# Dot products of the modulation held one behind each MLP unit, and four changes of where small and last data lie

## The chip, the core and the metric

The kernel runs on one core of one Trainium2 chip. The metric is the device time of one execution in microseconds (us), the median of several runs; lower is better. The core's engines each work through their own instructions in order: PE (TensorE, the matmuls), ACT (ScalarE), DVE (VectorE), POOL (GpSimd) and SP (SyncE), which here issues most of the DMA loads. The order of an engine's instructions is fixed when the program is built: a scheduler takes the instructions that the Python code traces and sets them one behind the other on each engine, by its own estimate of when each one's inputs are ready. An instruction whose input is late holds everything behind it on its engine.

## The reference: what is computed

Two layers of a token mixer and an MLP on x of 512 tokens by 1024, in fp32. What matters here:

```python
cond = silu(c)
for l in range(2):
    mod = cond @ mod_w[l] + mod_b[l]          # 1024 -> 6*1024
    shift1, scale1, gate1, shift2, scale2, gate2 = split(mod, 6)
    h = rms_norm(x, attn_pre_g) * (1 + scale1) + shift1
    y = mixers(h @ w_in) @ w_out              # sparse, retention, GLA and differential heads
    x = x + gate1 * rms_norm(y, attn_post_g)
    h = rms_norm(x, mlp_pre_g) * (1 + scale2) + shift2
    y = square(relu(h @ mlp_w1)) @ mlp_w2     # 1024 -> 4096 -> 1024
    x = x + gate2 * rms_norm(y, mlp_post_g)
```

## The kernel before

Each fp32 product is made of three matmuls (`mm3`) of a high and a low part: hi x hi, hi x lo, lo x hi. So every weight tile is loaded by SP into a ring of four buffers (`raw`), ACT rounds it into a high part (`act.copy`, line 267), and DVE or POOL subtracts that for the low part (line 268). `prep` does this; where the pair lies is set by the list `slots`, which is rotated: W6 is a pool of six pairs (`whi`, `wlo`) that lives through the whole kernel, WX ten pairs of a pool that is opened in `rest` (`xhi`, `xlo`) and closed at its end, WG eight pairs that share their place with the MLP's hidden tiles.

`mixers(l)` runs the input projections and the four head groups of layer l; at its start it opens a pool of ten pairs (`zh`, `zl`) on the side of the memory where WX was closed, and asks for the weights of the projections 3, 0 and 1, twelve tiles. `rest(l)` runs the output projection and the MLP. The MLP goes over the 4096 hidden columns in four quarters q. In a quarter there are eight hidden units f (24 matmuls of 512 columns each; quarter 0 has them in two halves of 256 tokens), each followed by relu (ACT), square (DVE, line 1325) and a split into high (ACT) and low (DVE) part in `hidden`; then eight output units (two column halves c by four token blocks b), each read out of PSUM by ACT (quarter 0) or added on DVE. The last quarter's output units come in an order of their own (`last`), and their weights are called `ws`: column half 0 from `slots`, column half 1 into the place of the MLP's input (`wr`). Behind each block of it come the post norm (`add_block`) and the norm ahead of the next layer (`norm_block`, `turn_half`).

The products `cond @ mod_w` are done on DVE: 96 dot products over 128 x 1024 (`gemv`, line 285), 16 at the start and 80 from a list `todo`, from which `fill(n)` takes n at a place in the program. Each loads 512 KB of `mod_w` (`gw`, two buffers) by SP. `fence` holds instructions behind which the dot products are set on DVE; in `rest` it holds the last subtraction of `turn_half`, from the beginning of the MLP on. All but eight of the 56 that layer 0's `rest` takes belong to layer 1, and all of them are done in layer 0. When the eighth of part 2 or 5 is done, `gain_out` turns the norm weights by PE (line 507), copies them to SBUF by ACT (line 509) into a buffer of the tag `sq`, and POOL issues a DMA of them to DRAM (line 510). The two `sq` buffers also serve `rope` (its products `r1` and `r2`), `headnorm` and `turn_half`.

Projection 3 gives keys, index keys, values, index weights and the GLA gate input; `ev_k` copies them out of PSUM with four ACT instructions a block, into `tmK`, `Va`, `wi` (scaled) and `ca`.

Of the kernel before, what the change touches and what calls it, by code (L numbers as in the profile page):

```python
# [10 lines left out]
F32 = mybir.dt.float32  # L11
# [4 lines left out]
ALU = mybir.AluOpType  # L16
# [73 lines left out]
P = 128  # L90
L = 2
DM = 1024
T = 512
KT = 8
NB = 4
# [103 lines left out]
def tile_trunk(ctx: ExitStack, tc: tile.TileContext, a, out, dbg=None):  # L199
    nc = tc.nc  # L200
    pe, act, dve, pool, sp = nc.tensor, nc.scalar, nc.vector, nc.gpsimd, nc.sync

    def bits(t):
        return t.bitcast(F32)
# [28 lines left out]
    ones = cp.tile([P, P], F32, name="ones")  # L233
# [13 lines left out]
    nt = ctx.enter_context(tc.tile_pool(name="nt", bufs=2))  # L247
# [5 lines left out]
    slots = [(wp, "whi", "wlo", WB)]  # L253
# [25 lines left out]
    fence = []  # L279
# [21 lines left out]
    def fill(n):  # L301
        for _ in range(min(n, len(todo))):
            todo.pop(0)()
# [157 lines left out]

    def split(v, hi, lo, eng=None):
        act.copy(hi, v)
        (eng or dve).tensor_tensor(lo, v, bits(hi), ALU.subtract)

    def h_tiles(name):
        a, b = (hp.tile([P, KT, T], F32R, name=f"{name}{s}", tag="h" + s, bufs=1) for s in "hl")
        whole[name] = (a, b)
        return [(a[:, i], b[:, i]) for i in range(KT)]
# [33 lines left out]
    def gain_out(l, which):  # L503

        gain(l, which)
        pt = tr.tile([P, T], F32, name=f"tg_{which}{l}", tag="tr")[0:KT, 0:P]
        pe.transpose(pt, gmul[l, which], ident)
        g = nt.tile([P, T], F32, name=f"gt_{which}{l}", tag="sq")[0:KT, 0:P]
        act.copy(g, pt)
        pool.dma_start(rows[2 * l + (which == "post2")], g)  # L510

# [95 lines left out]
    def mixers(l, h, ch):  # L607
# [38 lines left out]
        def pv_block(ps, b, ss, Vs, name):  # L646

            W = P * (b + 1)
            st = []
            for hh in range(2):  # L650
                pt = tr.tile([P, T], F32, name=f"tp{name}_{hh}", tag="tr")
                for j in range(b + 1):
                    pe.transpose(pt[:, P * j:P * j + P], ss[hh][:, P * j:P * j + P], ident)
                st.append(mx.tile([P, T], F32, name=f"pt{name}_{hh}", tag="PT", bufs=4))
                act.copy(st[hh][:, :W], pt[:, :W])
            for j in range(b + 1):
                for hh in range(2):
                    pe.matmul(ps[64 * hh:64 * hh + 64, b * P:(b + 1) * P], Vs[hh](j), st[hh][:, P * j:P * j + P],
                              start=(j == 0), stop=(j == b))
# [80 lines left out]
            ahead(3)  # L740


        Va = mx.tile([P, NB, 64], F32, name=f"Va{l}")
        wi = mx.tile([P, NB, 8], F32, name=f"wi{l}")
        ca = mx.tile([P, NB, 17], F32, name=f"ca{l}")
        pool.memset(ca[:, :, 16:], 1.0)
        tmK = [s0.tile([P, P], F32, name=f"tK{l}_{b}", tag="tK", bufs=4) for b in range(NB)]
        KS = mx.tile([P, 4, T], F32R, name=f"KS{l}")

        def ev_k(b, ps):  # L750
            act.copy(tmK[b][:, 0:128], ps[:, 0:128])
            act.copy(Va[:, b, :], ps[:, 128:192])
            act.mul(wi[:, b, :], ps[:, 192:200], 8 ** -0.5 * 64 ** -0.5)
            act.copy(ca[:, b, 0:16], ps[:, 200:216])

        def keys(b):
            rope(mx, tmK[b].rearrange("p (h d) -> p h d", d=64), "A", b, 2, f"K{l}_{b}", E[PLAN["kr"][b]])
# [317 lines left out]
        def a_block(pr, b):  # L1075
            if b:
                top(max(0, 16 * b + 1 - taken[0]))
            W = P * (b + 1)
            sb = []
            for hh in range(2):  # L1080
                nme = f"A{l}_{pr}_{hh}_{b}"
                ps = sc.tile([P, T], F32, name="s" + nme, tag="sc")
                two_pass(ps, QS[:, 2 * pr + hh, b * P:(b + 1) * P], 0, max(W, 256))
                s, rc = softmax_scores(ps[:, :W], masks[b], W, HD ** -0.5, nme)
                z = PLAN["xa"][4 * pr + b]
                xx = act.mul(s, s, rc) if z == "a" else E[z].tensor_scalar(s, s, rc, None, ALU.mult)
                if PLAN['fence']:
                    fence[:] = [xx]
                sb.append(s)
            yield  # L1090
            if b == 0:
                yh[pr] = yp.tile([P, T], F32, name=f"ya{l}_{pr}", tag="yp")
            pv_block(yh[pr], b, sb, [lambda j: Va[:, j, :]] * 2, f"A{l}_{pr}_{b}")
            if b == NB - 1:
                headnorm(pr, yh[pr])

# [171 lines left out]
    def rest(l, yv):  # L1268
# [12 lines left out]
        row = gain_row(l, "post1")  # L1281
        gain(l, "pre2")
        if l == 0:
            gemv_list((0, 5), *[(1, part) for part in range(6)])
        slots[:] = [W6] * 6 + [WG] * 8 + [WX] * 2
        wo = [[None] * KT for c in range(2)]
        for c in range(2):
# [33 lines left out]
        def hidden(ps, hid, c, name):  # L1321
            n = c.stop - c.start
            rl = nt.tile([P, T], F32, name=f"rf{name}", tag="rs", bufs=RS)[:, :n]
            act.activation(rl, ps, AF.Relu)  # L1324
            dve.tensor_tensor(rl, rl, ps, ALU.mult)  # L1325
            split(rl, hid[0][:, c], hid[1][:, c])

        full = slice(0, T)
        for q in range(4):
            hid = [tuple(ml.tile([P, T], F32R, name=f"hd{l}_{q}_{f}{s}", tag="g" + s, bufs=8) for s in "hl")  # L1330
                   for f in range(8)]
            ws = [None] * 8
            for half in range(2 if q == 0 else 1):
                c = cs(half) if q == 0 else full
                for f in range(8):
                    if half == 0:
                        ws[f] = prep_k(a["w1"][l, 8 * q + f], {"p": pool, "d": dve}[PLAN["w1lo"][f % len(PLAN["w1lo"])]] if q == 0 else dve)
                    ps = acc(f"pf{l}_{q}_{f}_{half}", c.stop - c.start)
                    for k in range(KT):
                        mm3(ps, ws[f][k], (h[k][0][:, c], h[k][1][:, c]), k == 0, k == KT - 1)  # L1340
                    hidden(ps, hid[f], c, f"{l}_{q}_{f}_{half}")
                    if (q, half, f) == (0, 0, 5):
                        turn(1)
                    fill(1 if q else 0)
            if q == 0:
                y = y_blocks(f"ym{l}")
            if q < 3:
                for c in range(2):
                    wk = [prep(a["w2"][l, q, c, k], [P, T]) for k in range(KT)]
                    for b in range(NB):  # L1350
                        ps = acc(f"p2{l}_{q}_{c}_{b}", T)
                        for k in range(KT):
                            mm3(ps, (hid[k][0][:, tb(b)], hid[k][1][:, tb(b)]), wk[k], k == 0, k == KT - 1)
                        if q == 0:
                            act.copy(y[b][:, c], ps)
                        else:
                            dve.tensor_tensor(y[b][:, c], y[b][:, c], ps, ALU.add)
                        fill(2)
        fill(len(todo))
        row = gain_row(l, "post2")  # L1360

        wr = h_tiles(f"wr{l}_")
        ws = [[prep(a["w2"][l, 3, 0, k], [P, T]) for k in range(KT)],
              [prep(a["w2"][l, 3, 1, k], [P, T], place=wr[k]) for k in range(KT)]]
        last = [(0, 0), (0, 1), (1, 0), (1, 1)]
# [60 lines left out]
```

## Time and profile before

| | us |
|---|---|
| median of 3 runs (lowest, highest) | 1480.65 (1478.78, 1491.46) |
| the profiled execution | 1477.14 |
| its span, first to last instruction | 1475.3 |
| PE busy in the span | 1406.2 |
| DVE busy | 961.5 |
| ACT busy | 725.7 |
| POOL busy | 213.6 |

Times in rows are microseconds from the start of the span unless marked ns. "Busy" is time in which an engine has an instruction under way; for PE that is no measure of speed, since its matmuls overlap one another and last longer at a lower clock. The granted clock is a share of TensorE's upper level of 2.4 GHz, so 0.50 is its lower level of 1.2 GHz. A row of the timeline gives start, duration, engine, line, operation, out<-in by tile names, shapes and count, and in brackets how long the engine stood idle before it and what ended that.

### The profile page before, as it was taken

Reading aid. Unit: us, or ns where it says so; the run is one execution under the profiler, and the core shown is the slowest. Engines: PE = TensorE matmul, PEld = TensorE weight load, DVE = VectorE, ACT = ScalarE, POOL = GpSimd, SP = SyncE. Lnnn points to the kernel's source line nnn. Section 1 sums busy time; section 2 is a strip of 40 time slices with the busy share of each in tenths; the row PEclk is TensorE's granted clock in tenths of the full one; section 3 lists DMA queues with packets and bytes.
Section 4 is the critical chain, followed back from the end, with each engine's and each line's share of the span. In section 5 each row is a group of like instructions: output and inputs, shape, how many; then the busy total and the mean of one; then the engine's idle time right before and its main releaser. Section 6 shows DMA issues by size and latency. Waiting matters only on the chain.

```text
span 1475.3 us, 21830 instructions
## 1 busy us (share of the span) xinstructions
PE 1406.2 (95%) x7754; PEld 1139.5 (77%) x7754; DVE 961.5 (65%) x2177; ACT 725.7 (49%) x1625; POOL 213.6 (14%) x212
## 2 busy tenths in 40 slices
PE   8889889999999989999999899999999999999998
PEld 6576867867898868888878768787689888888886
DVE  8999967777785877434565999764666334353444
ACT  5577467655542323323356575856756433242331
POOL 2434420420000000000002534213200000000000
PEclk9999999999999989999999999999999999999999
DMA  9530221455177876323231202211442332242311
GB/s 360 184 111 21 87 86 41 147 171 185 58 262 250 276 242 232 93 75 97 82 126 51 74 8 80 72 44 44 134 137 66 109 116 82 85 116 86 107 37 58
DMA packets 79062, 173.13 MB, mean 117 GB/s; under 512 B 9124, under 2 KB 11878, under 8 KB 78696
## 3 DMA queue, kind: packets, MB, share of 16 engines
q1 hardware_dynamic: 77348, 167.47, 35.1%
q0 software_dynamic: 1280, 4.21, 0.8%
q8 instruction: 61, 1.00, 0.3%
q14 instruction: 49, 0.40, 0.1%
q10 hardware_dynamic: 324, 0.04, 0.0%
HBM read 167.48 MB, written 4.21 MB: 116 GB/s over the span
## 4 chain that ended last, share of the span: by engine, by line
PE 66%; DVE 18%; DMA 7%; ACT 5%; issue 3%; POOL 1%; DVEq 0%; SPq 0%; ACTq 0%; POOLq 0%
PE pf L273 7%; PE p L272 7%; PE p L274 7%; PE pf L274 7%; PE p L273 7%; PE pf L272 7%; DMA gw<-modw 4%; PE ptm L272 3%; DVE ia L845 2%; PE ptm L273 2%; PE ptm L274 2%; DVE m L844 2%; DMA raw<-w 2%; PE po L273 1%; PE po L272 1%
## 5 line engine op out<-in xcount | busy, mean ns | idle before, releaser
L267 ACT CAST whi<-raw 128x512 fp32r<-128x512 f32 x372 | 228.1, 621 | 306.6 <-PE p L274 121.3
L268 DVE TENSOR_TENSOR wlo<-raw,whi 128x512 fp32r<-128x512 f32 x284 | 196.5, 703 | 138.3 <-ACT whi L267 135.3
L272 PE MATMUL pf<-h_h,whi 128*128 128x512 f32 (+1 forms) x640 | 221.9, 349 | 1.1 <-ACT h_h L558 1.1
L274 PE MATMUL pf<-h_h,wlo 128*128 128x512 f32 (+1 forms) x640 | 222.6, 348 | 0.0
L273 PE MATMUL pf<-h_l,whi 128*128 128x512 f32 (+1 forms) x640 | 222.3, 348 | 0.1
L272 PE MATMUL ptm<-whi,h_h 128*128 128x256 f32 x592 | 175.9, 298 | 3.0 <-ACT qc L887 1.4
L273 PE MATMUL ptm<-wlo,h_h 128*128 128x256 f32 x592 | 171.1, 290 | 1.5 <-DVE wlo L268 1.5
L274 PE MATMUL ptm<-whi,h_l 128*128 128x256 f32 x592 | 171.3, 290 | 0.4 <-DVE h_l L559 0.3
L268 POOL TENSOR_TENSOR wlo<-raw,whi 128x512 fp32r<-128x512 f32 x88 | 115.8, 1334 | 217.4 <-ACT whi L267 178.5
L272 PEld LDWEIGHTS pf<-h_h,whi 128*128 128x128 f32 x640 | 119.9, 188 | 18.5 <-ACT h_h L558 1.9
L273 PEld LDWEIGHTS pf<-h_l,whi 128*128 128x128 f32 x640 | 120.4, 188 | 17.3 <-DVE h_l L559 0.5
L274 PEld LDWEIGHTS pf<-h_h,wlo 128*128 128x128 f32 x640 | 120.4, 188 | 16.8
L285 DVE CUSTOM_DVE_ANT_0 gw<-gw,cond 128x1024 f32<-128x1024 f32 x80 | 100.4, 1257 | 46.1 <-DMA gw<-modw 46.0
L272 PEld LDWEIGHTS ptm<-whi,h_h 128*128 128x128 f32 x592 | 115.0, 194 | 11.6 <-issue 6.5
L273 PEld LDWEIGHTS ptm<-wlo,h_h 128*128 128x128 f32 x592 | 114.9, 194 | 7.3 <-issue 4.8
L274 PEld LDWEIGHTS ptm<-whi,h_l 128*128 128x128 f32 x592 | 114.9, 194 | 4.2 <-issue 3.2
L1325 DVE TENSOR_TENSOR rf<-rf,pf 128x512 f32<-128x512 f32 (+1 forms) x80 | 45.9, 575 | 35.1 <-ACT rf L1324 35.0
L1324 ACT ACTIVATE rf<-pf 128x512 f32<-128x512 f32 (+1 forms) x80 | 40.6, 507 | 41.2 <-PE pf L274 41.2
L844 DVE MAX8 m<-ia 128x8 f32<-128x256 f32 (+2 forms) x96 | 53.0, 554 | 1.3
L272 PE MATMUL po<-whi,yT_h 128*128 128x512 f32 x128 | 51.4, 404 | 0.6 <-ACT whi L267 0.6
L845 DVE MATCH_REPLACE8 ia<-m,ia 128x256 f32<-128x256 f32 (+2 forms) x96 | 51.9, 541 | 0.0
L948 ACT COPY QF<-q 32x256 f32<-32x256 f32 x120 | 48.4, 403 | 5.5 <-DVE q L925 1.2
(487 smaller groups left out, 3013.9 us busy)
## 6 DMA issues: line engine op xcount, KB each, us to landing
raw<-w SPq DMA_DIRECT2D x256, 256.0 KB, 2.9
gw<-modw SPq DMA_DIRECT2D x80, 512.0 KB, 4.3
raw<-wtm SPq DMA_DIRECT2D x76, 256.0 KB, 2.8
gs<-modw SPq DMA_DIRECT2D x16, 512.0 KB, 7.1
raw<-wo SPq DMA_DIRECT2D x32, 256.0 KB, 2.7
raw<-wtc SPq DMA_DIRECT2D x24, 256.0 KB, 2.8
xin<-xT SPq DMA_DIRECT2D x8, 256.0 KB, 4.7
wq<-wtm SPq DMA_DIRECT2D x8, 256.0 KB, 7.4
```

The costliest lines, as they stand in the source:

```text
L267: act.copy(hi, raw)
L268: (lo_eng or dve).tensor_tensor(lo, raw, bits(hi), ALU.subtract)
L272: pe.matmul(ps, l[0], r[0], start=start, stop=False)
L273: pe.matmul(ps, l[0], r[1], start=False, stop=False)
L274: pe.matmul(ps, l[1], r[0], start=False, stop=stop)
L285: return dve.tensor_tensor_reduce(raw, raw, cond, 1.0, 0.0, ALU.mult, ALU.add, modT[l][:, c:c + 1])
L844: dve.max(m8, acc)
L845: dve.match_replace(acc, m8, acc, MARK)
L948: f(Q[r, :, hd, :], QS4[c // 2][r, 2 * (c % 2):2 * (c % 2) + 2, :])
L1324: act.activation(rl, ps, AF.Relu)
L1325: dve.tensor_tensor(rl, rl, ps, ALU.mult)
```

## The change

Five edits, of which the last is in two places:

1. In the MLP `fence` is set anew by every hidden unit (its low-part subtraction) and by every output unit that DVE adds, so that a dot product taken by `fill` stands behind that unit on DVE. `fill` takes one in every second hidden unit of the second half of quarter 0, one per output unit (before: two), and one per hidden unit from quarter 1 on, as before.
2. The eight dot products of layer 1's part 5 move from layer 0's `rest` to layer 1's.
3. `gain_out` copies into the first rows of the constant tile `ones`, which nothing uses any longer by then, rather than into an `sq` buffer.
4. `Va`, `wi` and `ca` become one tile; `ev_k` copies 88 columns at once, and the scaling of `wi` moves to POOL.
5. The weights of the last quarter's hidden units go to WX for f below 4 and to W6 from 4 on; of the last quarter's output weights of column half 0, two go to WX and six to W6 (before: all eight to WX).

```diff
--- before.py
+++ after.py
@@ -461,7 +461,7 @@
 
     def split(v, hi, lo, eng=None):
         act.copy(hi, v)
-        (eng or dve).tensor_tensor(lo, v, bits(hi), ALU.subtract)
+        return (eng or dve).tensor_tensor(lo, v, bits(hi), ALU.subtract)
 
     def h_tiles(name):
         a, b = (hp.tile([P, KT, T], F32R, name=f"{name}{s}", tag="h" + s, bufs=1) for s in "hl")
@@ -505,7 +505,7 @@
         gain(l, which)
         pt = tr.tile([P, T], F32, name=f"tg_{which}{l}", tag="tr")[0:KT, 0:P]
         pe.transpose(pt, gmul[l, which], ident)
-        g = nt.tile([P, T], F32, name=f"gt_{which}{l}", tag="sq")[0:KT, 0:P]
+        g = ones[0:KT, :]
         act.copy(g, pt)
         pool.dma_start(rows[2 * l + (which == "post2")], g)
 
@@ -740,18 +740,17 @@
             ahead(3)
 
 
-        Va = mx.tile([P, NB, 64], F32, name=f"Va{l}")
-        wi = mx.tile([P, NB, 8], F32, name=f"wi{l}")
-        ca = mx.tile([P, NB, 17], F32, name=f"ca{l}")
+        Va = mx.tile([P, NB, 89], F32, name=f"Va{l}")
+        wi = Va[:, :, 64:72]
+        ca = Va[:, :, 72:89]
         pool.memset(ca[:, :, 16:], 1.0)
         tmK = [s0.tile([P, P], F32, name=f"tK{l}_{b}", tag="tK", bufs=4) for b in range(NB)]
         KS = mx.tile([P, 4, T], F32R, name=f"KS{l}")
 
         def ev_k(b, ps):
             act.copy(tmK[b][:, 0:128], ps[:, 0:128])
-            act.copy(Va[:, b, :], ps[:, 128:192])
-            act.mul(wi[:, b, :], ps[:, 192:200], 8 ** -0.5 * 64 ** -0.5)
-            act.copy(ca[:, b, 0:16], ps[:, 200:216])
+            act.copy(Va[:, b, 0:88], ps[:, 128:216])
+            pool.tensor_scalar(wi[:, b, :], wi[:, b, :], 8 ** -0.5 * 64 ** -0.5, None, ALU.mult)
 
         def keys(b):
             rope(mx, tmK[b].rearrange("p (h d) -> p h d", d=64), "A", b, 2, f"K{l}_{b}", E[PLAN["kr"][b]])
@@ -1090,7 +1089,7 @@
             yield
             if b == 0:
                 yh[pr] = yp.tile([P, T], F32, name=f"ya{l}_{pr}", tag="yp")
-            pv_block(yh[pr], b, sb, [lambda j: Va[:, j, :]] * 2, f"A{l}_{pr}_{b}")
+            pv_block(yh[pr], b, sb, [lambda j: Va[:, j, 0:64]] * 2, f"A{l}_{pr}_{b}")
             if b == NB - 1:
                 headnorm(pr, yh[pr])
 
@@ -1281,7 +1280,9 @@
         row = gain_row(l, "post1")
         gain(l, "pre2")
         if l == 0:
-            gemv_list((0, 5), *[(1, part) for part in range(6)])
+            gemv_list((0, 5), *[(1, part) for part in range(5)])
+        else:
+            gemv_list((1, 5))
         slots[:] = [W6] * 6 + [WG] * 8 + [WX] * 2
         wo = [[None] * KT for c in range(2)]
         for c in range(2):
@@ -1323,13 +1324,16 @@
             rl = nt.tile([P, T], F32, name=f"rf{name}", tag="rs", bufs=RS)[:, :n]
             act.activation(rl, ps, AF.Relu)
             dve.tensor_tensor(rl, rl, ps, ALU.mult)
-            split(rl, hid[0][:, c], hid[1][:, c])
+
+            fence[:] = [split(rl, hid[0][:, c], hid[1][:, c])]
 
         full = slice(0, T)
         for q in range(4):
             hid = [tuple(ml.tile([P, T], F32R, name=f"hd{l}_{q}_{f}{s}", tag="g" + s, bufs=8) for s in "hl")
                    for f in range(8)]
             ws = [None] * 8
+            if q == 3:
+                slots[:] = [WX] * 8 + [W6] * 8
             for half in range(2 if q == 0 else 1):
                 c = cs(half) if q == 0 else full
                 for f in range(8):
@@ -1341,7 +1345,7 @@
                     hidden(ps, hid[f], c, f"{l}_{q}_{f}_{half}")
                     if (q, half, f) == (0, 0, 5):
                         turn(1)
-                    fill(1 if q else 0)
+                    fill(1 if q else half * (f % 2))
             if q == 0:
                 y = y_blocks(f"ym{l}")
             if q < 3:
@@ -1354,12 +1358,13 @@
                         if q == 0:
                             act.copy(y[b][:, c], ps)
                         else:
-                            dve.tensor_tensor(y[b][:, c], y[b][:, c], ps, ALU.add)
-                        fill(2)
+                            fence[:] = [dve.tensor_tensor(y[b][:, c], y[b][:, c], ps, ALU.add)]
+                        fill(1)
         fill(len(todo))
         row = gain_row(l, "post2")
 
         wr = h_tiles(f"wr{l}_")
+        slots[:] = [WX] * 2 + [W6] * 6
         ws = [[prep(a["w2"][l, 3, 0, k], [P, T]) for k in range(KT)],
               [prep(a["w2"][l, 3, 1, k], [P, T], place=wr[k]) for k in range(KT)]]
         last = [(0, 0), (0, 1), (1, 0), (1, 1)]
```

## Rows read from the trace of the kernel before

**Rows 1.** The page, part 1: busy us (share of the span) xinstructions of each engine.

```profile
PE 1406.2 (95%) x7754; PEld 1139.5 (77%) x7754; DVE 961.5 (65%) x2177; ACT 725.7 (49%) x1625; POOL 213.6 (14%) x212
```

**Rows 2.** Stretch: length, busy us (xinstructions) by engine; clock; DMA share, GB/s.

```profile
475.34:519.69 44.35, 44.35 (x193) 36.01 (x192) 35.72 (x62) 15.51 (x28) 0.00 (x0) 1.00 0.81 271
519.69:574.66 54.97, 48.30 (x195) 37.22 (x194) 37.94 (x65) 12.66 (x22) 0.52 (x1) 0.91 0.74 246
619.01:664.04 45.03, 45.03 (x195) 36.08 (x194) 14.86 (x22) 9.87 (x17) 0.52 (x1) 1.00 0.23 73
```

**Rows 3.** Timeline of PE, ACT and DVE, 524 to 533.

```profile
527.02 0.80 PE L272 MATMUL p<-whi,hd_6h 128*128 128x512 f32 x1 [2.95 <-ACT hd_6h L463]
...
532.64 0.79 PE L272 MATMUL p<-whi,hd_7h 128*128 128x512 f32 x1 [3.72 <-ACT hd_7h L463]
...
531.96 0.62 ACT L463 CAST hd_7h<-rf 128x512 fp32r<-128x512 f32 x1 [3.46 <-DVE rf L1325]
...
529.26 1.23 DVE L285 CUSTOM_DVE_ANT_0 gw<-gw,cond 128x1024 f32<-128x1024 f32 x1 [0.60 <-DMA gw<-modw]
...
531.25 0.68 DVE L1325 TENSOR_TENSOR rf<-rf,pf 128x512 f32<-128x512 f32 x1
```

**Rows 4.** Line 285, 430 to 580: duration ns min/median/max; its waits (us, times).

```profile
L285 DVE CUSTOM_DVE_ANT_0 gw<-gw,cond x48: 1216/1225/1227, 434.7 to 577.9; 128x1024 f32<-128x1024 f32 x48
...
  DMA gw<-modw: 40.8, 35
```

**Rows 5.** Timeline of DVE and PE, 206 to 215.

```profile
212.61 0.19 DVE L595 TENSOR_TENSOR r2A<-tA,ssA 128x32 f32<-128x32 f32 x1 [2.13 <-DMA rows<-gt_post]
...
208.07 0.63 PE L691 MATMUL thA<-ident,hlA 128*128 128x128 f32 x4 [1.38 <-DVE hlA L687]
...
214.33 0.63 PE L691 MATMUL thA<-ident,hlA 128*128 128x128 f32 x4 [3.67 <-DVE hlA L687]
```

**Rows 6.** A stretch as in Rows 2, behind that wait.

```profile
216.00:222.00 6.00, 5.62 (x28) 3.99 (x27) 2.74 (x9) 3.74 (x9) 0.00 (x0) 0.50 0.41 169
```

**Rows 7.** Timeline of PE and ACT where layer 1 begins, 755 to 764.

```profile
756.44 0.51 PE L272 MATMUL ptm<-whi,h_h 128*128 128x256 f32 x2 [1.24 <-ACT whi L267]
757.99 0.45 PE L273 MATMUL ptm<-wlo,h_h 128*128 128x256 f32 x1 [1.04 <-DVE wlo L268]
...
762.72 0.62 ACT L267 CAST whi<-raw 128x512 fp32r<-128x512 f32 x1 [3.34 <-DMA raw<-wtm]
763.25 0.20 ACT L492 ACTIVATE rsp<-msp 128x1 f32<-128x1 f32 x1
```

**Rows 8.** Stretches as in Rows 2, where layer 1 begins.

```profile
756.00:762.00 6.00, 4.51 (x23) 4.30 (x24) 4.68 (x13) 3.38 (x10) 0.54 (x1) 0.72 0.65 226
...
768.00:784.00 16.00, 13.77 (x104) 12.11 (x103) 11.05 (x29) 11.42 (x30) 5.28 (x4) 1.00 0.63 194
784.00:800.00 16.00, 15.91 (x129) 14.91 (x127) 6.74 (x23) 7.42 (x22) 4.21 (x4) 1.00 0.05 12
```

**Rows 9.** Timeline of ACT and PE behind layer 0's last hidden unit.

```profile
713.31 1.22 ACT L267 CAST wr_h<-raw 128x512 fp32r<-128x512 f32 x2 [1.47 <-DMA raw<-w]
715.32 0.62 ACT L267 CAST wr_h<-raw 128x512 fp32r<-128x512 f32 x1 [0.78 <-DMA raw<-w]
...
708.39 0.39 PE L272 MATMUL p<-whi,hd_0h 128*128 128x512 f32 x1
...
714.01 0.39 PE L272 MATMUL p<-wr_h,hd_0h 128*128 128x512 f32 x1
```

**Rows 10.** POOL's groups by shape, then the timeline of POOL and DVE at 51.6.

```profile
L442 POOL TENSOR_SCALAR ssA<-rt 128x32 f32<-128x32 f32 x1 | 0.4, 362 | 23.0 <-ACT rt L423 23.0
...
51.59 1.28 POOL L268 TENSOR_TENSOR wlo<-raw,whi 128x512 fp32r<-128x512 f32 x1 [0.59 <-ACT whi L267]
...
51.67 1.24 DVE L596 TENSOR_TENSOR r2K<-tK,ssA 128x16 f32<-128x16 f32 x1
```

**Rows 11.** Timeline of SP's queue: start, time from the first issue to the last's end.

```profile
438.09 17.21 SPq L283 DMA_DIRECT2D gw<-modw  x7
```

## The prediction

> **What bounds the kernel now.** Read the page's first part first: PE is busy in 1406.2 us of the span of 1475.3, DVE in 961.5 [rows 1]. So nothing is to be had from making another engine shorter on average; what can be had is the time in which PE stands or runs at its lower clock. The second view is therefore the table of stretches. In the MLP it is cut at the output units of a quarter, eight units of 24 matmuls, the same work each time: 45.03 us in quarter 2, but 54.97 in quarter 1, at a mean clock of 0.91 [rows 2]. That is 9.94 us lost in one place. The timeline says where: two matmuls wait, 2.95 us for the high part of hidden tile 6 and 3.72 us for that of tile 7 [rows 3], and the rest of the 9.94 is the lower clock that follows. The copy for tile 7 on ACT in turn waits 3.46 us for DVE's square of that unit, and on DVE a dot product stands ahead of that square, itself waiting for its load (529.26, 0.60 us for the DMA) [rows 3]. So PE waits for ACT, ACT for DVE, and DVE for 512 KB of `mod_w`.
>
> It is no single accident. In quarter 1's hidden units DVE is busy 35.72 of 44.35 us [rows 2], and from 430 to 580 it stood 40.8 us in 35 waits for such loads, around 48 dot products of 1.225 us [rows 4]. Two of them passed per hidden unit there, since the old fence stands far ahead and holds none back; DVE fell behind unit by unit, until the hidden tiles were late for the output units. Quarter 2's output units run without dot products and DVE is busy 14.86 us of 45.03 [rows 2].
>
> Two smaller losses follow from the same reading. At 212.61 a `rope` product waits 2.13 us for the DMA of the turned norm weights, which holds its `sq` buffer, and PE stands 3.67 us [rows 5]; the 6 us from 216 run at 0.50 with PE busy 5.62 [rows 6]. And where layer 1 begins, PE waits 1.24 and 1.04 us for the first projection weights [rows 7]: 23 matmuls in the 6 us from 756, and 104 in the 16 us from 768, against 129 in the 16 us after that [rows 8].
>
> **Dot products behind their units, eight moved to layer 1 (edits 1 and 2).** The dot products stay 96 of 1.225 us. What goes is the stall: 54.97 - 45.03 = 9.94 us. What is late next is nothing that I can find: with one dot product a unit, DVE has in a hidden unit the square and the split's low part, two low parts of weights and one dot product, 4 x 0.7 + 1.3 = 4.1 us (0.68 from the square's row [rows 3]; 1.3 with the reading of the sum) in a unit of 44.35 / 8 = 5.54 us; before it had 5.4 and the waits. An output unit has one fewer 0.7. Layer 0 needs 48 dot products and the new places are 4 + 8 + 16 + 16 + 4, so the last stands in quarter 3; the eight of layer 1 take 4 + 4 places of its quarter 0. Eight of 1.225 us are 9.8 us on DVE, which I cost at nothing: in a quarter's output units without dot products DVE idles 30.2 us [rows 2]. Without that cover they would cost up to the 9.8. The added wait: a dot product stands behind the unit's subtraction, and behind the dot product stand the next unit's square and weights. It costs nothing while its load has landed, and the load has two units, 11 us, for a buffer that is free again two dot products earlier. Value 9.94; the bounds are 8 (some wait left) and 9.94.
>
> **Own place for the norm weights (edit 3).** The DVE wait of 2.13 us [rows 5] goes in full, since nothing else holds `ones`. The half-clock stretch cost up to half of 5.62 us, 2.8 [rows 6]. PE would still stand some 1.5 us there (3.67 - 2.13), close to the 1.38 us at 208.07 [rows 5], after which PE did not yet run at half clock; so the fall may be spared. Bounds 2.1 and 4.9; I take the middle, 3.5, because PE is not the pace of all of those 6 us. The other three times that the weights are turned lie in the MLP, where nobody takes an `sq` buffer: nothing.
>
> **Where the last weights lie (edit 5).** WX gives its place to the next mixers' ten pairs. Before, all eight last weights lay there until the last unit, ending at about 755.1, so nearly all of the first twelve loads could be rounded only then. After, eight WX pairs are free from quarter 3's fourth unit on, so most of projections 3 and 0 can be ready early, when ACT and DVE have time. One of the ten new pairs also reaches over a low part of a hidden tile of the MLP's pool and must still wait for the last unit. What the stage loses now, at the rate of 129 matmuls in 16 us [rows 8]: 1 us from the last unit's end to 756, then 25 matmuls of 48 missing in 6 us, 3.1 us, and 25 missing in the 16 us from 768, 3.1 us; 7.2 in all. The second 3.1 is the last token block's norm: its logarithm (763.25) stands on ACT behind a rounding that waited 3.34 us for its load [rows 7]. That goes. Whether the first 4.1 goes hangs on the one pair that still waits. Bounds 2.4 and 7.2; I take 4.0, nearer to the lower end for that pair.
>
> This edit also costs. In W6 the last six weights wait for hidden units 5, 6 and 7, so the ring of four raw buffers is held by them. Now the fifth weight of column half 1 is rounded at 713.31 and the seventh at 715.32, both waiting for the DMA [rows 9], and unit (0,1) begins at 714.01 [rows 9], 24 matmuls or 5.6 us behind 708.39. After, the ring holds two weights of half 0 and only two of half 1 when unit 7 ends, so each weight of half 1 comes two places later: the seventh and eighth about when the ring comes round once more, 2.8 us after a buffer is free. By that count the eighth is ready at some 719.8 and wanted at 718.9 to 719.1: 0.5 to 1 us of stall, in each layer. Value -1.8 for both; bounds 0 and -4.
>
> **Fewer key copies (edit 4).** Eight small ACT copies and eight scalings leave ACT, and eight scalings of 128x8 come to POOL. ACT's share I cost at nothing: DVE and not ACT is behind there. The POOL operation is not in the trace; the nearest row is 0.362 us for 128x32 [rows 10]. Its readers come 20 us later, so as work it is hidden. But a DVE product of 128x16 that began 0.08 us after a POOL subtraction took 1.24 us and ended as that did [rows 10]: a DVE operation can be held by a POOL one. So four in layer 0, where DVE is the pace, cost between nothing and 4 x 0.362 = 1.4 us; I take 0.5. The Trainium skill's page "SBUF — State Buffer", section "SBUF: two separate sides", speaks against this edit in the same sense: a DVE instruction with two SBUF inputs and a GpSimd instruction that reads SBUF take a shared port pair by turns, and the second waits for the whole of the first. The row agrees, with 1.24 us. By that rule each of the four costs up to its whole length, which is the upper bound above.
>
> **Sum.** 9.94 + 3.5 + 4.0 - 1.8 - 0.5 = 15.1 us. From the profiled execution, 1477.14, that gives 1462.0; the median of the three runs lies 3.5 us above that execution, so the forecast as a median is 1465.5.
>
> **Rivals.** (a) Only the stall goes. The pair that still waits keeps PE waiting at layer 1's start and then at the low clock, the last weights cost their bound, POOL its bound, the norm weights give the wait alone: 9.94 + 2.1 + 0 - 4 - 1.4 = 6.6, 1474.0. For it: ACT's and DVE's order where layer 1 begins is fixed at build time by estimates that evidently put the first rounding behind other work. Chance 0.25.
> (b) The hold doesn't hold: a dot product behind unit f is still ahead of the square of unit f+1, and if its load is late the same wait comes back. Then 15.1 - 9.9 = 5.2, 1475.4. Against it: half as many loads in a unit. Chance 0.05.
> (c) Everything at its good end: 9.94 + 4.9 + 7.2 = 22, 1458.6. Chance 0.14.
> (d) Slower. A load of `mod_w` stands at the head of SP's queue until a held dot product has freed its buffer, and the weights behind it stand too. SP has spent 17.21 us over seven such loads already [rows 11], without harm, as weights were loaded well ahead. If the lead is used up, some 40 held units each keep PE waiting; at a tenth of a unit, 0.55 us, that is 22 us, 1487.5. It decides from the point at which a weight lands later than its unit begins. Chance 0.04.
>
> **How the numbers follow.** The forecast (1462 to 1469) has 0.52. A measurement of this kernel tells about 1% from no change, which is 14.8 us, or 1465.8: the forecast lies on that line. Faster by more: half of the forecast's 0.52, somewhat more for its middle, and (c), 0.44. Slower by more: (d), 0.04. Within: 0.52. The range from 1458.5 to 1475 takes in (a) and (c) and leaves out (b) and (d).
>
> **What would show it.** Right: quarter 1's output units last 45 us at a clock of 1.00; the `rope` product waits for no `rows` DMA; the first rounding for layer 1 lies before 755 in its place, and the last block's logarithm waits for no load. Wrong: waits of PE for hidden tiles, or for `wr` in unit (0,1); a first matmul of layer 1 that still waits for `whi`; waits of PE for `whi` all through the MLP, with SP standing at `gw`.

## The result, and the profile after

The changed kernel takes 1464.82 us (median of 4 runs, 1462.85 to 1466.83), the kernel before on the same chip 1481.2 (1478.78 to 1491.46): a ratio of 0.9881, 95% interval 0.9855 to 0.9907. The prediction was 1465.5. The two profiled executions differ by less: 1477.14 before, 1466.83 after. So of a gain of 16.4 us the two traces show only 10.3; where the rest lies is the experiments' first question.

The page's first part and the stretches that answer to [rows 1, 2] are these: quarter 1's hidden units, then its eight output units.

```profile
PE 1405.3 (96%) x7754; PEld 1139.6 (78%) x7754; DVE 961.8 (66%) x2177; ACT 726.3 (50%) x1609; POOL 219.4 (15%) x220
...
472.02:516.38 44.36, 44.36 (x193) 36.01 (x192) 29.55 (x48) 19.34 (x34) 0.00 (x0) 1.00 0.59 188
516.38:561.45 45.07, 45.07 (x194) 36.21 (x193) 23.49 (x40) 9.18 (x15) 0.00 (x0) 1.00 0.49 169
```

The engines are as busy as before; the output units last 45.07 us at a clock of 1.00, where they took 54.97 at 0.91. DVE has 48 instructions in the hidden units instead of 62, and PE waits for no hidden tile. The timeline of DVE in the output units shows the new order, and line 285 from 427 to 575 (cf. [rows 4]) what became of the waits for loads:

```profile
533.45 0.69 DVE L1361 TENSOR_TENSOR ym<-ym,p 128x512 f32<-128x512 f32 x1 [3.79 <-PE p L274]
534.05 1.22 DVE L285 CUSTOM_DVE_ANT_0 gw<-gw,cond 128x1024 f32<-128x1024 f32 x1
...
535.20 2.49 DVE L268 TENSOR_TENSOR wlo<-raw,whi 128x512 fp32r<-128x512 f32 x4
...
L285 DVE CUSTOM_DVE_ANT_0 gw<-gw,cond x26: 1218/1219/1229, 430.0 to 569.7; 128x1024 f32<-128x1024 f32 x26
...
  DMA gw<-modw: 9.4, 6
```

One dot product stands behind each unit and the weights behind it: 26 of them in place of 48. Six of the 26 still wait for their load, 9.4 us in all instead of 40.8, and no matmul waits for it.

The stretch around the norm weights (cf. [rows 5, 6]), DVE first, then PE:

```profile
206.21 0.18 DVE L595 TENSOR_TENSOR r2A<-tA,ssA 128x32 f32<-128x32 f32 x1
...
206.31 0.63 PE L691 MATMUL thA<-ident,hlA 128*128 128x128 f32 x4 [2.25 <-DVE hlA L687]
...
209.71 1.05 PE L691 MATMUL thA<-ident,hlA 128*128 128x128 f32 x4
```

The second `rope` product waits for no DMA and stands 6.4 us earlier than at 212.61, 1.1 us of which is the earlier start of the whole stretch (180.32 against 181.38); the second group of transposes starts 3.4 us behind the first instead of 6.3, with no wait.

Where layer 1 begins (cf. [rows 7]), ACT and then PE:

```profile
742.51 0.60 ACT L267 CAST whi<-raw 128x512 fp32r<-128x512 f32 x1
...
749.50 0.62 ACT L267 CAST whi<-raw 128x512 fp32r<-128x512 f32 x1 [3.40 <-DMA raw<-wtm]
750.03 0.20 ACT L492 ACTIVATE rsp<-msp 128x1 f32<-128x1 f32 x1
...
743.17 0.51 PE L272 MATMUL ptm<-whi,h_h 128*128 128x256 f32 x2 [1.26 <-ACT whi L267]
744.72 0.39 PE L273 MATMUL ptm<-wlo,h_h 128*128 128x256 f32 x1 [1.04 <-DVE wlo L268]
```

Nothing has changed but the time at which it happens: the last unit ends at 741.91, the first rounding still comes after it, PE waits 1.26 and 1.04 us as it did 1.24 and 1.04, and the last block's logarithm still stands behind a rounding that waits 3.40 us for its load (3.34 before).

Unit (0,1) (cf. [rows 9]) begins at 700.75. ACT's last four roundings of its eight weights, and the stretches of PE up to it and through it:

```profile
700.57 1.22 ACT L267 CAST wr_h<-raw 128x512 fp32r<-128x512 f32 x2 [0.87 <-DMA raw<-w]
...
702.58 1.37 ACT L267 CAST wr_h<-raw 128x512 fp32r<-128x512 f32 x2 [0.17 <-DMA raw<-w]
```

```profile
695.10:701.50 6.40, 6.40 (x29) 5.11 (x29) 4.94 (x8) 4.74 (x9) 0.00 (x0) 1.00 0.59 176
701.50:707.10 5.60, 5.60 (x26) 4.49 (x25) 3.73 (x7) 2.15 (x5) 0.00 (x0) 1.00 0.76 258
```

The last two of the eight are rounded by 703.95, 3.2 us behind the unit's start, and PE stays busy throughout.

### The profile page after: what moved, and what is told of

Same layout as the page of the kernel before. It is cut to its first block, busy times and chain, and to the rows that moved or that the text cites. A ratio compares the mean times of both kernels' runs of the same rounds, so it can differ in the third digit from the quotient of the medians.

```text
span 1465.1 us, 21801 instructions
## 1 busy us (share of the span) xinstructions
PE 1405.3 (96%) x7754; PEld 1139.6 (78%) x7754; DVE 961.8 (66%) x2177; ACT 726.3 (50%) x1609; POOL 219.4 (15%) x220
## 4 chain that ended last, share of the span: by engine, by line
PE 74%; DVE 17%; ACT 4%; issue 2%; DMA 2%; POOL 1%; SPq 0%; DVEq 0%; ACTq 0%; POOLq 0%
PE pf L273 8%; PE pf L274 8%; PE pf L272 8%; PE p L274 8%; PE p L272 8%; PE p L273 8%; PE ptm L272 3%; DVE ia L844 3%; PE ptm L273 2%; PE ptm L274 2%; DVE m L843 2%; PE po L273 1%; PE po L274 1%; PE po L272 1%; DVE gs L285 1%
## 5 line engine op out<-in xcount | busy, mean ns | idle before, releaser
L273 PEld LDWEIGHTS pf<-h_l,whi 128*128 128x128 f32 x640 | 120.4, 188 | 17.2 <-DVE h_l L559 0.5
```

Of the source, the lines that this page charges most:

```text
L273: pe.matmul(ps, l[0], r[1], start=False, stop=False)
```

## The experiments

In the table each stage is read from PE's timeline of one profiled execution: "mixers 0" ends at the first matmul of layer 0's output projection, "norm place" lies between two fixed matmuls of its middle (some 181 to 227 in the kernel before), "q1 out" are the eight output units of quarter 1, "MLP 0" the whole MLP of layer 0, "start 1" runs from its last unit's end to one fixed matmul of layer 1. The ratio is that of the times to the kernel before on the same chip. The runs stand on more than one chip, with medians of 1481.63, 1481.95 and 1479.39 us for the kernel before in the experiments, so medians from two chips can differ by that alone, and the ratio stands beside them.

| kernel | median us (runs) | ratio, 95% | mixers 0 | norm place | q1 out | MLP 0 | start 1 |
|---|---|---|---|---|---|---|---|
| before | 1481.2 (4) | 1 | 333.8 | 45.5 | 55.1 | 372.7 | 53.3 |
| before, again | 1485.93 (1) | | 342.0 | 47.3 | 54.4 | 372.1 | 53.7 |
| changed | 1464.82 (4) | 0.9881 [0.9855, 0.9907] | 330.2 | 41.4 | 45.1 | 362.9 | 54.2 |
| changed, again | 1464.72 (6) | 0.9883 [0.9858, 0.9908] | 332.1 | 41.6 | 45.1 | 362.9 | 53.4 |
| hold alone | 1471.5 (6) | 0.9930 [0.9902, 0.9957] | 341.2 | 45.5 | 45.1 | 363.0 | 54.0 |
| all but the hold | 1473.58 (12) | 0.9945 [0.9928, 0.9962] | 330.4 | 41.4 | 55.0 | 372.5 | 53.5 |
| old norm place | 1469.15 (6) | 0.9907 [0.9882, 0.9931] | 334.1 | 45.7 | 45.1 | 362.9 | 53.3 |
| old key copies | 1467.42 (6) | 0.9892 [0.9869, 0.9915] | 334.3 | 42.4 | 45.1 | 362.8 | 53.3 |
| old slots | 1464.89 (6) | 0.9879 [0.9855, 0.9904] | 332.0 | 41.5 | 45.1 | 363.0 | 53.4 |
| fences, old numbers | 1467.13 (6) | 0.9902 [0.9879, 0.9925] | 329.4 | 41.5 | 46.6 | 366.2 | 53.6 |
| new numbers, no fence | 1476.84 (12) | 0.9978 [0.9963, 0.9992] | 330.5 | 41.4 | 56.5 | 374.0 | 54.2 |
| nine pairs | 1464.3 (6) | 0.9883 [0.9856, 0.9910] | 329.1 | 41.5 | 45.1 | 362.8 | 54.3 |
| nine pairs, one norm first | 1464.39 (6) | 0.9885 [0.9863, 0.9907] | 332.6 | 40.8 | 45.1 | 362.8 | 52.3 |
| nine pairs, both norms first | 1463.14 (6) | 0.9875 [0.9849, 0.9901] | 330.6 | 41.5 | 45.1 | 362.8 | 52.5 |

**The changed kernel again**, with nothing altered.

> The changed kernel once more, with nothing altered. It asks how large the gain is: the two profiled executions differ by 10.3 us (1477.14 and 1466.83), the medians by 16.4 us (1481.2 and 1464.82). If the traces tell the whole gain, this run gives a difference of medians of 10 to 12 us; if there is something that the profiled execution of the kernel before happened not to show, 14 to 18 us again. It also asks whether the small losses of the profiled execution in layer 1 (1.6 us near 940, 1.2 us between 1063 and 1111) are the kernel's or that execution's: if the kernel's, they stand in this trace too, within 0.3 us.

Measured: 1464.72, against 1481.63 (17 runs): 16.9 us. The gain that the pair of traces doesn't show is real. The small losses in layer 1 were the one execution's: from the last unit to the next output projection it was 306.0 us there and 304.1 here (304.2 before).

**The kernel before again**, for a second trace.

> The kernel before once more, for a second trace of it. Its profiled execution took 1477.14 us, 4.5 us under the median of 17 runs, 1481.63, while those of the changed kernel lie at their median. Theory: where the lower clock falls in the mixers differs from one execution to the next, and that execution met few such stretches (11.7 us of full-clock time lost in 8-us stretches under 0.97, against 15.0 to 17.0 in four other traces). Then a second trace shows the same waits, but 3 to 8 us more in stretches of the mixers at a lower clock. Rival: the wait for the norm weights' DMA is what differs; then the rope product behind it waits over 4 us here, against 2.13 us.

Stretches of the first and the second trace, each between the same matmuls (58.60 and 59.40 the tenth key transpose; 181.38 and 186.32 the norm place), then DVE and PE of the second at the norm weights:

```profile
58.60:120.57 61.97, 51.27 (x319) 40.96 (x319) 60.37 (x147) 42.87 (x99) 29.16 (x30) 0.97 0.37 120
181.38:226.86 45.48, 38.88 (x243) 31.88 (x245) 30.26 (x116) 30.20 (x87) 10.66 (x9) 0.89 0.24 77
```

```profile
59.40:125.47 66.07, 55.58 (x319) 45.25 (x319) 60.15 (x147) 43.23 (x98) 29.38 (x30) 0.90 0.34 114
186.32:233.57 47.25, 40.97 (x244) 33.88 (x246) 30.30 (x116) 30.33 (x87) 10.68 (x9) 0.83 0.22 73
...
218.62 0.19 DVE L595 TENSOR_TENSOR r2A<-tA,ssA 128x32 f32<-128x32 f32 x1 [2.11 <-DMA rows<-gt_post]
...
220.34 1.08 PE L691 MATMUL thA<-ident,hlA 128*128 128x128 f32 x4 [3.65 <-DVE hlA L687]
```

The same 319 matmuls take 61.97 us at a mean clock of 0.97 and 66.07 at 0.90, with DVE and ACT as busy; the wait for the norm weights is 2.11 us again. The theory holds, if a little over its 3 to 8 us, and the rival doesn't: one instruction stream differs by 8.8 us in its time (1477.14 and 1485.93), 8.2 of them in "mixers 0", and what differs is where stretches of the mixers run at the lower clock. What decides that no run here shows. The profiled execution of before met few.

**The hold alone** (edits 1 and 2; edits 3 to 5 undone) and **all but the hold** (edits 3 to 5). The diff is the second's, against the changed kernel:

```diff
-            gemv_list((0, 5), *[(1, part) for part in range(5)])
-        else:
-            gemv_list((1, 5))
+            gemv_list((0, 5), *[(1, part) for part in range(6)])
...
-            fence[:] = [split(rl, hid[0][:, c], hid[1][:, c])]
+            split(rl, hid[0][:, c], hid[1][:, c])
...
-                    fill(1 if q else half * (f % 2))
+                    fill(1 if q else 0)
...
-                            fence[:] = [dve.tensor_tensor(y[b][:, c], y[b][:, c], ps, ALU.add)]
-                        fill(1)
+                            dve.tensor_tensor(y[b][:, c], y[b][:, c], ps, ALU.add)
+                        fill(2)
```

> The dot products held and spread (edits 1 and 2) alone, with the norm weights, the last weights and the key copies as before. Theory: the hold removes the stall and nothing else: 9.9 us under the kernel before, some 1471.3 where the kernel before has 1481.2, and quarter 1's output units of layer 0 last 45 us at a clock of 1.00. Rival: the stall of quarter 1 also needs the other edits' earlier arrival; then the eight output units last over 48 us here and the gain is under 6 us.

> The other three edits (norm weights, last weights, key copies) without the held dot products. Theory by the traces: 3.3 us stay up to the last quarter of layer 0 and some 0.4 us to the end, so 0 to 4 us under the kernel before, and the eight output units of quarter 1 last 53 to 56 us again at a clock near 0.91. Rival: the three edits carry the 6 us by which the medians differ more than the traces do; then it is 5 to 7 us under the kernel before.

Quarter 1's output units in the one, then in the other with the second wait of PE:

```profile
527.40:572.50 45.10, 45.10 (x194) 36.21 (x193) 23.55 (x40) 9.21 (x15) 0.00 (x0) 1.00 0.52 168
```

```profile
515.70:570.70 55.00, 47.60 (x195) 36.89 (x194) 37.68 (x65) 12.66 (x22) 0.52 (x1) 0.94 0.75 244
...
528.55 0.79 PE L272 MATMUL p<-whi,hd_7h 128*128 128x512 f32 x1 [3.66 <-ACT hd_7h L463]
```

The hold removes the stall by itself: 10.1 us by the medians. But the other three edits are worth 8.1 us together, not 0 to 4: more even than the rival's 5 to 7. The table shows where: "mixers 0" lasts 329.1 to 332.6 us in the nine traces that have edits 3 and 4, and 333.8, 341.2 and 342.0 in the three that have neither. 10.1 and 8.1 make 18.2, near the 16.9 of the whole.

**Fences with the old numbers** (two dot products behind an output unit, all 56 in layer 0), and **the new numbers without fences**: in the diff above, only the lines with `fill` and `gemv_list` undone, or only those with `fence`.

> The changed kernel with the number of dot products behind each unit as before (one in a hidden unit, two in an output unit, all 56 in layer 0), but each held behind its unit. Theory: the hold is what removes the stall; quarter 1's hidden units then have one dot product each, its output units two, and the eight output units last 45 us at a clock of 1.00, so the time is that of the changed kernel, 1464 to 1466. Rival: it is the smaller number per unit that removes it; then the eight output units last over 50 us and the time is 1470 or over.

> The changed kernel with its smaller numbers (one dot product behind each unit, eight moved to layer 1) but without the hold: nothing ties a dot product to its unit. Theory: without the hold they slip forward, two into each hidden unit of quarter 1, DVE falls behind as before, and the eight output units last 51 to 56 us: 1471 to 1475. Rival: with fewer of them DVE keeps up; the output units last 45 to 47 us and the time is 1465 to 1467.

With fences, quarter 1's output units and PE's only wait in them; without, the same units and DVE's dot products from 427 to 575:

```profile
515.70:562.20 46.50, 45.21 (x195) 36.06 (x194) 30.73 (x54) 9.40 (x16) 0.52 (x1) 1.00 0.71 225
...
544.28 0.27 PE L507 MATMUL tg_post<-ident,g_post 128*8 128x128 f32 x1 [1.29 <-DVE g_post L311]
```

```profile
515.70:572.20 56.50, 48.89 (x194) 37.88 (x193) 33.79 (x58) 13.02 (x22) 0.00 (x0) 0.91 0.61 199
...
L285 DVE CUSTOM_DVE_ANT_0 gw<-gw,cond x40: 1215/1226/1229, 428.4 to 548.3; 128x1024 f32<-128x1024 f32 x40
...
  DMA gw<-modw: 33.3, 27
```

The hold is the cause, though both times lie over their theory's range, 1467.13 with fences alone by 1.1 us and 1476.84 without fences by 1.8. Without the hold fewer dot products are no help: layer 0's are all done by 548 instead of 578, as crowded as before, and the kernel is 3 to 5 us slower than with all but the hold (1476.84 against 1473.58; 0.9978 against 0.9945). Of that 1.5 us lie in MLP 0 (374.0 against 372.5); the rest stays open. With the hold the smaller numbers are worth some 3 us: with two behind a unit, PE's transpose of the norm weights waits for DVE, 1.29 us here and 0.64 and 1.20 in the other output stages, and MLP 0 takes 366.2 us instead of 362.9. The fence is set anew in two places, by hidden units and by output units; no run parts them.

**The old norm place** (edit 3 undone):

```diff
-        g = ones[0:KT, :]
+        g = nt.tile([P, T], F32, name=f"gt_{which}{l}", tag="sq")[0:KT, 0:P]
```

> The changed kernel with the turned norm weights in their sq buffer again (edit 3 undone). Theory by the traces: the stretch from 205 to 222 costs 3.2 us more and stays, so 1467 to 1469 where the changed kernel has 1464.7. Rival 1: the low clock behind that wait differs from one execution to the next and the edit is worth the 4.9 us of its upper bound or more: 1470 or over. Rival 2: PE's wait there is only passed on, and nothing reaches the end: 1464 to 1466.

The stretch with the old place, then POOL's DMA, the `rope` product and the transposes; below it the same stretch of the changed kernel:

```profile
181.50:227.20 45.70, 36.83 (x240) 30.35 (x241) 34.15 (x119) 30.04 (x87) 9.84 (x9) 0.93 0.23 75
...
209.81 0.76 POOL L510 DMA_DIRECT2D rows<-gt_post  x1
...
212.73 0.19 DVE L595 TENSOR_TENSOR r2A<-tA,ssA 128x32 f32<-128x32 f32 x1 [0.43 <-DMA rows<-gt_post]
...
215.31 0.63 PE L691 MATMUL thA<-ident,hlA 128*128 128x128 f32 x4 [4.46 <-DVE hlA L687]
```

```profile
180.30:221.70 41.40, 36.46 (x239) 30.64 (x240) 32.93 (x119) 29.54 (x87) 9.82 (x9) 0.92 0.24 82
```

4.4 us by the medians, 3.6 by the ratios (0.9907 against 0.9883, in 1481) and 4.3 by the stretch (45.7 against 41.4): the theory, whose 3.2 us and 1469 are passed by a little. The clock is the same in the two stretches, 0.93 and 0.92, and PE stands 8.87 us of the one and 4.94 of the other, so nearly all of the price is standing. In the table all four traces with the old place have 45.5 to 47.3, all ten with the new one 40.8 to 42.4. The wait for the DMA is only 0.43 us here and the price is the same: the `rope` product stands 2.9 us behind the issue of that DMA (in the kernel before 2.8, issued at 209.78) wherever it falls, while with its own place it runs at 206.21, ahead of the issue.

**The old key copies** (edit 4 undone: four ACT instructions a block, nothing on POOL).

> The changed kernel with the key copies as before (edit 4 undone). Theory: the 3.3 to 4.4 us won between 66 and 74 are given back to 1.1 to 2 by 180, so the kernel is 1 to 2 us slower than the changed one: 1465.7 to 1466.7. Rival 1: what was won early stays, and is most of the 6 us by which the medians differ more than the traces: 1469 to 1471. Rival 2, the prediction's: a scaling on POOL holds DVE, and without it the kernel is 0 to 1.4 us faster.

ACT's first rounding of a key and PE's second start of key transposes, with the old copies and then with the new:

```profile
53.69 0.59 ACT L766 CAST hlk<-tK 128x128 fp32r<-128x128 f32 x2
...
56.37 0.44 PE L771 MATMUL thk<-ident,hlk 128*128 128x128 f32 x2 [0.97 <-DVE hlk L767]
```

```profile
52.08 0.30 ACT L765 CAST hlk<-tK 128x128 fp32r<-128x128 f32 x1
...
54.43 0.55 PE L770 MATMUL thk<-ident,hlk 128*128 128x128 f32 x3 [0.83 <-DVE hlk L766]
```

With the old copies the first rounding follows the last of ACT's sixteen; with the new ones it stands ahead of the last block's. It begins 1.6 us earlier, and these transposes 1.9 us (the very first, 53.33 against 54.14, 0.8 us); 0.5 of each is the later start of the execution with the old copies (the instructions before the copies stand 0.5 us later). The medians say 2.7 us, the ratios 1.3 (0.9892 against 0.9883, in 1481), and their intervals overlap. But "mixers 0", 334.3, lies over all nine traces with the new copies and the new norm place (329.1 to 332.6): a gain of 1 to 3 us, the theory's 1 to 2 or somewhat more, and not the cost that the prediction set. The exact size stays open, since this part of the mixers is where executions differ most by the clock.

**The old slots** (edit 5 undone).

> The changed kernel with the last weights where they lay before (edit 5 undone). Theory: the edit gains nothing where layer 1 begins, because its first pair waits for the last unit, and costs nothing in unit (0,1): 1464 to 1466. Rival, the prediction's terms: without it 4.0 us are lost where layer 1 begins and 1.8 us won in the units (0,1): 1466 to 1468.

1464.89, and MLP 0 363.0 against 362.9, "start 1" 53.4 against 53.4 and 54.2. The edit neither gains nor costs: the theory.

**Nine pairs**, to find out why:

```diff
-        slots[:] = [(s0, "zh", "zl", 10)] * 10 + [(wp, "whi", "wlo", WB)] * 2
+        slots[:] = [(s0, "zh", "zl", 9)] * 9 + [(wp, "whi", "wlo", WB)] * 3
```

> The changed kernel with nine pairs of the mixers' pool in place of ten, and three of the other pool in place of two, so that the mixers' pool no longer reaches over the MLP's hidden tiles. Theory: the one pair that reached over a low part of a hidden tile, and was handed out first, held the first rounding for layer 1 until the last unit, and the eleven behind it stood in the same line; without it the first roundings lie before the last unit's end, the first matmul of layer 1 waits less than 0.3 us, no rounding waits over 3 us for its load, and the time is 3 to 6 us under the changed kernel. Rival 1: the roundings come early but the stage is paced by the norm of the last token block; then the first wait goes (1.3 us) and no more than 2 us come to the end. Rival 2: the loads, not the place, are late; then nothing changes, within 1 us.

The two stretches of 6 us from the last unit's end, first with ten pairs (the changed kernel), then with nine, with the ninth rounding, the logarithm behind it and PE's next wait:

```profile
741.91:747.91 6.00, 3.70 (x29) 3.49 (x30) 5.45 (x14) 4.19 (x12) 0.98 (x3) 1.00 0.55 172
747.91:753.91 6.00, 4.32 (x35) 3.91 (x33) 3.72 (x11) 3.64 (x11) 1.67 (x2) 1.00 0.77 260
```

```profile
740.29:746.29 6.00, 6.00 (x53) 6.00 (x53) 5.97 (x15) 4.96 (x16) 1.75 (x3) 1.00 0.71 252
746.29:752.29 6.00, 2.36 (x20) 2.16 (x19) 2.61 (x13) 2.22 (x9) 0.60 (x1) 0.87 0.66 222
...
750.25 0.62 ACT L267 CAST whi<-raw 128x512 fp32r<-128x512 f32 x1 [3.75 <-DMA raw<-wtm]
750.78 0.20 ACT L492 ACTIVATE rsp<-msp 128x1 f32<-128x1 f32 x1
...
751.97 0.47 PE L770 MATMUL thk<-ident,hlk 128*128 128x128 f32 x1 [3.64 <-ACT hlk L765]
```

The first half of the theory holds: the first pair held all the others, and without it the roundings start at 736.07, before the last unit's end, and the first matmul waits for nothing (53 in 6 us instead of 29). The second half falls: the time is the same, 1464.3. Of the 24 matmuls won 15 are lost in the next 6 us (20 against 35) and the rest behind that ("start 1" 54.3 against 54.2): the ninth rounding now waits 3.75 us for its load at the head of ACT, and the rounding of a key, for which PE waits, and the norm of the last block stand behind it. In the time that is rival 1, though the wait at the head is one for a load. Whether the norm or the loads set the pace is the next question.

**Nine pairs, with the ninth to twelfth rounding put behind the last block's first norm on ACT, and behind both**: a dependency of order alone from that norm's exponential to the four roundings.

```diff
-        act.copy(hi, raw)
+        hold_back(act.copy(hi, raw))
...
+    def hold_back(cast): behind and behind.pop(0) and after(exps[-2], cast)
...
-            ahead(3)
+            behind[:] = [0] * 8 + [1] * 4; ahead(3)
```

(`exps` lists the exponentials of `rsqrt_mean`; -2 is the first norm of the last block, -1 the second.)

> Nine pairs, and the ninth to twelfth rounding for layer 1 put behind the last token block's first norm on ACT. With nine pairs alone the first wait was gone (the first matmul of layer 1 at 740.12, right behind the last unit), but the ninth rounding waited 3.75 us for its load and the last block's logarithm (750.78) stood behind it, though its input was there from 747.2. Theory: where layer 1 begins the last block's norm is the pace; 2 to 3.6 us are won over nine pairs alone, 1461 to 1462.5. Rival: the loads are the pace and what is won in the norm is lost for the weights of the next projection: 1464 to 1465.

> The same, with the four roundings behind both norms of the last token block, so that the key copies, too, stand ahead of them on ACT (with nine pairs PE waited 3.64 us for a key copy that stood behind the rounding). Theory: the last block's turned columns come 3 to 4 us earlier and PE's wait of 3.64 us goes; 3 to 5 us under nine pairs alone, 1459.5 to 1461.5. Rival: the four weights held back are those of the next projection, and PE waits for them instead, 2 to 6 us: 1464 to 1468.

PE's wait in the first of them; the logarithm, the four roundings and a later stretch in the second; last the same stretch of the changed kernel:

```profile
753.44 0.38 PE L272 MATMUL ptm<-whi,h_h 128*128 128x256 f32 x1 [1.94 <-ACT whi L267]
```

```profile
749.29 0.20 ACT L492 ACTIVATE rsp<-msp 128x1 f32<-128x1 f32 x1 [0.68 <-DVE msp L490]
...
753.91 2.16 ACT L267 CAST whi<-raw 128x512 fp32r<-128x512 f32 x4
...
754.12:768.12 14.00, 13.08 (x78) 11.56 (x77) 9.43 (x16) 8.66 (x17) 4.07 (x3) 0.76 0.45 142
```

```profile
753.91:767.91 14.00, 11.72 (x77) 10.55 (x78) 10.58 (x28) 11.04 (x27) 6.67 (x6) 0.88 0.70 214
```

Behind one norm, PE waits 1.94 us for the weights held back, and the time stays, 1464.39: the rival. Behind both, the wait of 3.64 us shrinks (PE's longest wait for a key rounding there is 1.70 us), but the 14 us from 754.12 run at 0.76, where the changed kernel had 0.88 from 753.91. In both traces "start 1" is some 2 us shorter than with nine pairs (52.3 and 52.5 against 54.3); the medians don't show that gain clear of noise, and two traces of the changed kernel differ by 0.8 there. 1463.14 is the lowest median of the study; its interval covers the changed kernel's ratio, so no version is shown to beat it, and what paces this stage stays open.

## Why the prediction was right, step by step

- **The stall, 9.94.** Right in place, cause and size: 54.97 became 45.07, and the hold alone took 10.1 off. That it is the hold and not the smaller numbers, which the prediction did not part, was shown by taking each alone. The reckoned load of DVE in a hidden unit, 5.4 us before and 4.1 after, was too high: the rows have 35.72 / 8 = 4.5 and 29.55 / 8 = 3.7, with 14 and 7 dot products in the eight units.
- **The moved eight and the added wait, nothing.** Right: MLP 1, where the eight now stand, is as before (360.7 us against 360.8), and the waits for loads fell to 9.4 us instead of growing. Rivals (b) and (d) did not come.
- **The norm weights, 3.5.** Measured 3.6 to 4.4, inside 2.1 to 4.9, but not in the two terms that made it up. The wait of 2.13 us was too small a measure: what costs is that the `rope` product had to stand behind a DMA at all, and with the old place that is 3.9 us more of PE's standing where the wait itself is 0.43. The other term, a fall of the clock that may be spared, is not seen: the two stretches run at 0.93 and 0.92.
- **Where the last weights lie, 4.0 gained and 1.8 lost.** Both wrong: nothing is gained and nothing lost. In the gain the step that failed is the place of one pair: the prediction named the pair that must wait for the last unit, and took it for one weight of twelve. It is handed out first, and the other eleven are rounded behind it, as nine pairs showed. Rival (a) had this right. "That goes", said of the last block's norm, failed too, since the load behind the ring of four came as late as before (3.40 us against 3.34); so two of the prediction's own signs of being right did not come. The count of the ring in unit (0,1) put the eighth weight 5.8 us behind the unit's start; its high part was there after 3.2 and PE had no wait. The two errors were of opposite sign and left 2.2 of 15.1, which is luck.
- **Key copies, -0.5.** Wrong in sign: "ACT's share I cost at nothing" failed, as ACT's copies stand ahead of the roundings that the key transposes wait for: the first rounding begins 1.1 us earlier without them. The POOL scalings of layer 0 took 0.56, 0.24, 0.23 and 0.23 us beside other work; what they shifted on DVE is told in the last section.
- **The sum.** By the runs 9.9 + 4.3 + 0 + (1 to 3) = 15.2 to 17.2, against 15.1 said and 16.4 to 16.9 measured. The stall, two thirds of it, was understood; that the rest came out is luck in part, since 2.2 too much for the last weights was made up by 0.8 too little for the norm weights and 1.5 to 3.5 too little for the key copies. Edits 3 to 5 together gave 8.1, one by one 5.3 to 7.3; the difference is within the intervals and stays open. The forecast hung on the median and not on the profiled execution alone, by adding the 3.5 us between them; that was right, for the trace of before had met fewer stretches at the lower clock than other executions do.

## What to carry to other kernels

Work that only fills gaps needs a place in the order of its engine, not only a number per step: without one it slides forward as far as its data allow and arrives in a lump. A pool that reaches over another one's last tiles by a single buffer is as late as that tile if the buffer is handed out first. Where a stage runs partly at the lower clock, one trace is one draw of where that falls; compare stages between fixed instructions over several traces before pricing an edit there.

## What the runs showed of the hardware beyond that

A DVE instruction's length beside POOL does not follow its own size. In the trace of before a sum of two 128x1 columns took 1.23 us, begun 0.06 us after a POOL subtraction of 128x512 (the first of two in its row); in the changed kernel's first key block the product that follows the two POOL scalings took 1.21 us, begun 0.11 us after the subtraction behind them:

```profile
61.95 2.61 POOL L268 TENSOR_TENSOR wlo<-raw,whi 128x512 fp32r<-128x512 f32 x2 [1.44 <-ACT whi L267]
...
62.01 1.23 DVE L1201 TENSOR_TENSOR nlam<-lex 128x1 f32<-128x1 f32 x1
```

```profile
51.03 0.88 POOL L753 TENSOR_SCALAR Va<-Va 128x8 f32<-128x8 f32 x2
51.99 1.27 POOL L268 TENSOR_TENSOR wlo<-raw,whi 128x512 fp32r<-128x512 f32 x1
...
52.10 1.21 DVE L594 TENSOR_TENSOR r1K<-tK,ccA 128x32 f32<-128x32 f32 x1
```

The Trainium skill's page "SBUF — State Buffer", section "SBUF: two separate sides", has the rule for it, the second instruction waiting out the whole of the first, and these rows agree. What the edit added there was not the length of a scaling (0.27 us in the median of the eight, 1.94 at the longest, in layer 1) but a shift of which product met the subtraction: r2K with 1.24 us before [rows 10], r1K after.
